# Hybrid attention and time-mix layer on one core: preparation steps joined on TensorE, attention's meta keys moved to the last key block, the next group's norm output reloaded by halves

## The chip, the core and the metric

The kernel runs on one core of a Trainium2 chip. The metric is the device time of one execution in microseconds (us). Three timed runs of the kernel before gave 2245.62, 2245.93 and 2246.27 us; the median, 2245.93 us, is the time before. PE is the TensorE engine, DVE VectorE, ACT ScalarE, POOL GpSimd, and SP the engine whose queue issues the DMAs.

## What is computed

One decoder layer over 1040 rows of width 1024: 16 meta rows are put ahead of 1024 input rows. A half-step SwiGLU FFN, a mixer, and a second half-step FFN follow each other, each behind an RMS norm. The mixer projects the normed rows once; one half of the columns feeds stick-breaking attention with 8 heads, the other an RWKV-7 time mix with 8 heads. All is fp32.

```python
h = h + 0.5 * swiglu(rms_norm(h, ffn1_norm), ...)
proj = rms_norm(h, mix_norm) @ w_in
sb_out = stick_breaking_attention(q, k, v)        # A[t,s] = sigmoid(z_ts) * prod_{s<j<t} (1 - sigmoid(z_tj))
rw_out = rwkv7_time_mix(proj[..., 3 * SB_WIDTH:]) # S = S * w + sa (kk*a) + v k ; y = S r ; per head norm, bonus, gate
h = h + concat([sb_out, rw_out]) @ w_out
h = h + 0.5 * swiglu(rms_norm(h, ffn2_norm), ...)
out = rms_norm(h, final_norm)[:, N_META:]
# in the time mix: kk = k * k_k, divided by its norm per head of 64 columns
```

## The kernel before, in words

Rows are worked on in two groups: group A holds the meta rows and the first 512 rows (528 columns, since the tensors lie transposed, depth on the partitions), group B the other 512. Every large product is made in three fp32r matmuls of high and low parts (`mm3`, L687: weights high by input high, high by low, low by high). A weight block of 512 KB is loaded into a ring of two raw buffers (`wraw`), split by ACT into its high part (`whi`) and by DVE into its low part (`wlo`), each in a ring of two. In the order of the program: FFN 1 on A, projections of A, FFN 1 on B, projections of B, output projection (`wout`, matmuls into `pwo`) of A, FFN 2 on A, output projection of B, FFN 2 on B. This is the dense work, and it keeps PE supplied.

The mixer's small work runs beside it. For each group there are four units of the time mix: two stretches of 256 or 320 rows by two pairs of heads. One unit goes through `prep` (L1373: low-rank products into `psw` and `psa`, sums of squares into `pss`, their reciprocal roots spread over the partitions by the transposes `pri`, decay factors, the products `pG`, the bonus `pb`, transposes `pT` and `pV`), `lanes` (L1568: POOL inverts 16x16 triangles into `T`; they go through memory by `Td` and `Nd` and come back by sixteen small loads into `t` and `tt`, then PE combines them: `pw`, `pp`, `pz`, `pe`), `chain` (L1657: the recurrence, 64 rows a step: `px`, `us`, `pu`, `rsv`) and `post`. Attention follows in `attn`: `attn_z` makes the weights, `attn_av` (L1897) transposes them by blocks of keys (`pat`), splits them (`ath`, `atl`) and multiplies by the values (`po`). The 16 meta keys are a block of their own, with which `attn_av` begins.

What sets the order: the whole program is written out by a planner (class `Clock`, L192). Each piece of work is a generator; where it yields, the planner may go on with another one, whichever can start earliest by the planner's own costs. So PE's order is a mix of dense work and small pieces, decided at build time; every engine then takes its instructions strictly in that order. On DVE, ACT, POOL and SP the planner picks, among pending instructions, the one that can start first, and among equals the one of higher level (`trace`, L314: URGENT, LOAD, PLAIN, LAZY; an instruction that is neither urgent nor a weight load or split has PLAIN). `prep` runs as a task of priority 6, `lanes` of 7, `chain` of 9. Where the planner sees an idle stretch on PE it can put in `warm` matmuls of the identity, which compute nothing that is kept.

`prep` and `post` share a ring of two PSUM banks (`G`, GB = 2). `need(..., bank=...)` waits for one free bank of a ring, `two(..., bank=...)` for both.

The norm output of group B is made early and parked in memory (`nbd`). When the projections of A have read a range of columns of the tiles `nh`, `nl` for the last time, `load_n1` (L2420) loads B's columns over them: two depth halves q (tiles numbered 144 and 146 for depth 0 to 511, 145 and 147 for the rest), a high and a low part each. `proj` (L1213) calls it after the last item of a range; the last three items of the projections go over the ranges (0, 256) and (256, 528) one after the other, so their weights are loaded twice.

All instructions are issued through one wrapper, so each has line L107 in the profile; they are told apart by the names of their tiles, out<-in.

Of the kernel before, what the change touches and what calls it, by code (L numbers as in the profile page):

```python
# [7 lines left out]
F32 = mybir.dt.float32  # L8
# [8 lines left out]
P = 128  # L17
# [8 lines left out]
C = 64  # L26
# [165 lines left out]
class Clock:  # L192
# [121 lines left out]
    def trace(self, eng, op, call, out, ins, k):  # L314
# [4 lines left out]
        lvl = self.LOAD if self.ahead else self.URGENT if self.urg > 0 else self.LAZY if self.urg < 0 else self.PLAIN  # L319
# [159 lines left out]
class Ker:  # L479
# [733 lines left out]
    def proj(self, items, g, before=None, after=None):  # L1213
# [7 lines left out]
        for i, (c0, c1) in enumerate(ranges):  # L1221
            if before:
                yield from before(i)
            for col0, ncol, evac in items:
                if i == 0 or len(items) > 1:
                    wh, wl = yield from load(col0, ncol)
                yield self.need(*[x[k][:, c0:c1] for k in range(KT) for x in (nh, nl)], bank=self.nextbank)
                ps = self.bank("pd")[0:ncol, :c1 - c0]
                for k in range(KT):
                    self.mm3(ps, wh[:, k, :], wl[:, k, :], nh[k][:, c0:c1], nl[k][:, c0:c1], k == 0, k == KT - 1)  # L1230
                    yield
                yield lambda: all(self.flags.get(("root", g, r)) for r in range(1 if c1 == 256 else 2))
                with self.urgent():
                    evac(ps, c0, c1)
# [116 lines left out]
    def projections(self, g, before, after):  # L1351
# [9 lines left out]
        yield from self.proj(sb[-NL:], g, None, after)  # L1361
# [11 lines left out]
    def prep(self, u, pr, out):  # L1373
# [37 lines left out]
        for e, hp in enumerate(hps):  # L1411
            nc.scalar.activation(sq[:, e, :], kS[:, e, :], AF.Square, scale=self.v("kk", hp))
        for e, hp in enumerate(hps):
            yield self.two(tw, bank=bank)
            pw, pa = G("psw")[:, :ns], G("psa")[:, :ns]
# [11 lines left out]
        blks = [(0, 0), (P, P), (ns - P, 2 * P)][:-(-ns // P)]  # L1427
        nq = 2 * len(blks)
        yield self.need(sq, bank=bank)
        ps = G("pss")  # L1430
        for e in range(2):
            for j, (t0, _) in enumerate(blks):
                k = 2 * (e * len(blks) + j)
                nc.tensor.matmul(ps[:, k:k + 2], lhsT=sq[:, e, t0:t0 + P], rhs=self.blk, start=True, stop=True)
        rt = rp.tile([P, 3, 2 * nq], F32, tag="rt", bufs=2, name="rt")
        ssv, rinv = rt[:, 0], rt[:, 1]
        V.tensor_copy(out=ssv, in_=ps[:, 0:2 * nq])
# [10 lines left out]
        for e, hp in enumerate(hps):  # L1448
            yield self.need(rw, bank=bank)
            ps = G("pri")[:, :ns]  # L1450
            for j, (t0, c0) in enumerate(blks):
                k = 2 * (e * len(blks) + j)
                rr = slice(c0 - t0, P)
                nc.tensor.transpose(out=ps[:, c0:t0 + P], in_=rw[rr, k:k + 2, :].rearrange("p a d -> p (a d)"), identity=self.ident[rr, rr])
            V.scalar_tensor_tensor(kkn[:, e, :], kS[:, e, :], self.v("kk", hp), ps, ALU.mult, ALU.mult)
# [66 lines left out]
        yield self.need(prod, bank=bank)  # L1522
        pb = G("pb")
        po = ns - 256
# [4 lines left out]
        bon = rp.tile([P, 8], F32, tag="bon", bufs=2, name="bon")  # L1529
        nc.scalar.activation(bon, pb[:, 0:8], AF.Copy)  # L1530

# [8 lines left out]

        rsv = rp.tile([P, 2, NC, 2, C], F32, tag="rsv", bufs=self.rb, name="rsv")
        vt = rp.tile([P, 4, P], F32, tag="vt", bufs=2, name="vt")
        b0 = NC - 4
        yield self.need(vS, bank=bank)
        pt = G("pV").rearrange("p (j t) -> p j t", t=P)
        for j in range(4):
            t0 = po + P * (j % 2)
            nc.tensor.transpose(out=pt[:, j, :], in_=vS[:, j // 2, t0:t0 + P], identity=self.ident)
        nc.scalar.activation(vt, pt, AF.Copy)
        for h in range(2):  # L1550
            ro = slice(64 - 64 * h, 128 - 64 * h)
            for e in range(2):
                nc.scalar.activation(rsv[ro, :, b0 + e:NC:2, h, :],
                                     pt[64 * e:64 * e + 64, :, 64 * h:64 * h + 64].rearrange("p (a b) t -> p a b t", a=2), AF.Copy)
        if b0:
            yield self.need(vS, bank=bank)
            pt = G("pV0").rearrange("p (j t) -> p j t", t=P)
            for e in range(2):
                nc.tensor.transpose(out=pt[0:64, e, :], in_=vS[:, e, 0:C], identity=self.ident)
            for h in range(2):  # L1560
                ro = slice(64 - 64 * h, 128 - 64 * h)
                nc.scalar.activation(rsv[ro, :, 0, h, :], pt[0:64, 0:2, 64 * h:64 * h + 64], AF.Copy)
# [334 lines left out]
    def attn_av(self, hp, pr, g, bufs, ops, att):  # L1897
# [10 lines left out]
        grps = [[0]] + [list(range(j, min(j + 2, nb - 1))) for j in range(1, nb - 1, 2)] + [[nb - 1]]  # L1908

        def tr(grp, h):  # L1910
            m = len(grp)
            pt = psa.tile([P, 2, 256], F32, tag="t", bufs=bufs["t"], name="pat")
            ath = ap.tile([P, 2, 256], F32R, tag="ath", bufs=bufs["at"], name="ath")
            atl = ap.tile([P, 2, 256], F32R, tag="atl", bufs=bufs["at"], name="atl")
            self.hold((ath, atl))
            ks = blocks[grp[0]][1]
            cs = slice(P, 256) if grp[0] == nb - 1 else slice(0, 256)
            for jj, j in enumerate(grp):
                s0 = blocks[j][0]
                for e in range(cs.start // P, 2):  # L1920
                    nc.tensor.transpose(out=pt[0:ks, jj, e * P:e * P + P], in_=att[e][h][:, s0:s0 + ks], identity=self.ident)
            self.split(ath[0:ks, 0:m, cs], atl[0:ks, 0:m, cs], pt[0:ks, 0:m, cs])
            return ath, atl, ks, cs

        def av(grp, hs):
            ks, cs = hs[0][2:]
            for jj, j in enumerate(grp):
                for h in range(2):
                    for x in range(2):
                        nc.tensor.matmul(po[:, h, cs], lhsT=vs[0:ks, j, h, :, :].rearrange("p a d -> p (a d)"),  # L1930
                                         rhs=hs[h][x][0:ks, jj, cs], start=(j + h + x == 0), stop=(j == nb - 1 and x == 1),
                                         skip_group_check=True)
            for x in hs:
                self.drop(x[0:2])

        def trs(grp):
# [3 lines left out]
            return grp, [tr(grp, h) for h in range(2)]  # L1940
        prev = yield from trs(grps[0])
        for grp in grps[1:] + [None]:

            yield self.need(*[x for hs in prev[1] for x in hs[0:2]])
# [170 lines left out]
    def body(self):  # L2115
# [300 lines left out]
        def dense():  # L2416
            ch = [(0, 512)]
            yield from firstA()

            def load_n1(i):  # L2420
                for q in range(2):
                    for j in range(2):
                        cs = slice(*chB[i])
                        with self.urgent():
# [116 lines left out]
```

## Time and profile before

| | |
|---|---|
| timed runs, median (lowest, highest) | 2245.93 us (2245.62, 2246.27) |
| the profiled execution's own time | 2247.88 us |
| its span, first to last instruction | 2246.0 us |
| DVE, ACT, POOL busy | 1547.6, 1096.6, 574.1 us |
| weight blocks loaded (512 KB each), five largest groups | 342 |
| mean granted PE clock | 0.997 |

A busy time is the union of an engine's instructions. Matmul ends are modelled and overlap, so the step from one matmul's start to the next tells what it costs, not its duration. In a timeline row the first number is the start, the second the time to the end of the merged instructions, and a bracket at the end gives the idle time before it with what ended it. A matmul on plain fp32 data counts as two instructions, one on fp32r data or a transpose as one.

### The profile page before, as it was taken

To read this page: it belongs to the slowest core of one execution; us is meant where nothing else is said; L and a number is where in the kernel's file an instruction comes from. 1 tells how busy PE (TensorE), PEld (TensorE's weight loads), DVE (VectorE), ACT (ScalarE), POOL (GpSimd) and SP (SyncE) were. 2 spreads that over 40 slices of the span, in tenths; PEclk is the share of its full clock that TensorE was granted. 3 is DMA by queue.
4 is the path that set the end of the run, shared out by engine and by line. 5 is a ranking of instruction groups with operands and counts; after the bars stand their busy time and mean duration, and the time that the engine had idled before them with its cause. 6 is when DMAs were issued, how large, how long until landed. Compare 5 with 4: busy or idle time off the path is not lost.

```text
span 2246.0 us, 41718 instructions
## 1 busy us (share of the span) xinstructions
PE 2218.6 (99%) x16409; PEld 1967.9 (88%) x16409; DVE 1547.6 (69%) x2633; ACT 1096.6 (49%) x2176; POOL 574.1 (26%) x722
## 2 busy tenths in 40 slices
PE   9999999999999999999999999999999999999998
PEld 8999999999878888778888988887878899899998
DVE  5887776476666655566576787556777656897774
ACT  5444444534444434655435564445656436455444
POOL 1321111013143231542012325314443101322120
PEclk9999999999999999999999999999999999999999
DMA  5543232545643232332556534334222433333332
GB/s 171 179 113 104 85 104 79 167 129 144 198 112 99 74 100 91 100 93 76 158 142 190 164 101 118 86 93 118 79 83 61 132 118 120 116 104 106 110 89 82
DMA packets 408730, 257.61 MB, mean 115 GB/s; under 512 B 45005, under 2 KB 392357, under 8 KB 408534
## 3 DMA queue, kind: packets, MB, share of 16 engines
q1 hardware_dynamic: 408534, 254.95, 39.3%
q8 instruction: 129, 2.11, 0.4%
q14 instruction: 67, 0.55, 0.1%
HBM read 220.90 MB, written 33.99 MB: 113 GB/s over the span
## 4 chain that ended last, share of the span: by engine, by line
PE 91%; DVE 3%; issue 2%; ACT 2%; DMA 1%; SPq 1%; POOL 0%; DVEq 0%; ACTq 0%; POOLq 0%
PE pd L107 33%; PE pu L107 21%; PE pg L107 21%; PE pwo L107 3%; PE px L107 3%; PE po L107 2%; PE pz L107 2%; PE pat L107 2%; DVE wlo L107 1%; SPq L107 1%; PE pG L107 1%; ACT whi L107 1%; PE psw L107 0%; PE pp L107 0%; DVE nl L107 0%
## 5 line engine op out<-in xcount | busy, mean ns | idle before, releaser
L107 ACT ACTIVATE whi<-wraw 128x1024 fp32r<-128x1024 f32 x314 | 330.7, 1053 | 324.7 <-PE pd L107 195.8
L107 DVE TENSOR_TENSOR wlo<-wraw,whi 128x1024 fp32r<-128x1024 f32 (+1 forms) x312 | 406.8, 1306 | 99.4 <-ACT whi L107 91.4
L107 PE MATMUL pd<-ah,whi 128*128 128x512 f32 (+2 forms) x944 | 323.8, 343 | 2.9 <-DVE h L107 2.0
L107 PE MATMUL pd<-ah,wlo 128*128 128x512 f32 (+2 forms) x944 | 319.3, 338 | 1.2 <-DVE wlo L107 1.2
L107 PE MATMUL pd<-al,whi 128*128 128x512 f32 (+2 forms) x944 | 317.8, 337 | 0.6 <-DVE al L107 0.3
L107 PE MATMUL pd<-nh,whi 128*128 128x256 f32 (+7 forms) x648 | 209.5, 323 | 0.0
L107 PE MATMUL pu<-nh,whi 128*128 128x512 f32 (+3 forms) x576 | 205.6, 357 | 0.0
L107 PE MATMUL pd<-nh,wlo 128*128 128x256 f32 (+7 forms) x648 | 204.3, 315 | 0.0
L107 PE MATMUL pd<-nl,whi 128*128 128x256 f32 (+7 forms) x648 | 203.4, 314 | 0.0
L107 PEld LDWEIGHTS pd<-ah,whi 128*128 128x128 f32 x944 | 177.5, 188 | 24.9 <-DVE h L107 3.4
L107 PE MATMUL pu<-nh,wlo 128*128 128x512 f32 (+3 forms) x576 | 197.9, 344 | 0.0
L107 POOL TENSOR_TENSOR qs<-wraw 128x512 f32<-128x512 f32 x64 | 106.1, 1660 | 358.1 <-DVE ql L107 133.5
L107 PE MATMUL pg<-nh,whi 128*128 128x512 f32 (+3 forms) x536 | 196.9, 367 | 0.8 <-ACT nh L107 0.6
L107 PE MATMUL pu<-nl,whi 128*128 128x512 f32 (+3 forms) x576 | 196.8, 342 | 0.0
L107 PEld LDWEIGHTS pd<-ah,wlo 128*128 128x128 f32 x944 | 177.5, 188 | 21.2 <-DVE wlo L107 2.1
L107 PEld LDWEIGHTS pd<-al,whi 128*128 128x128 f32 x944 | 177.6, 188 | 19.3 <-DVE al L107 2.0
L107 PE MATMUL pg<-nh,wlo 128*128 128x512 f32 (+3 forms) x536 | 188.7, 352 | 0.1
L107 PE MATMUL pg<-nl,whi 128*128 128x512 f32 (+3 forms) x536 | 187.6, 350 | 0.9 <-DVE nl L107 0.9
L107 DVE SCALAR_TENSOR_TENSOR h<-pd,h 128x256 f32<-128x256 f32 (+1 forms) x200 | 107.5, 541 | 76.7 <-PE pd L107 76.2
L107 POOL TENSOR_TENSOR al<-sl,ah 128x512 fp32r<-128x512 f32 (+2 forms) x45 | 73.5, 1632 | 317.7 <-ACT ah L107 314.6
L107 PEld LDWEIGHTS pd<-nh,whi 128*128 128x128 f32 (+2 forms) x648 | 120.1, 185 | 11.8 <-issue 3.1
L107 PEld LDWEIGHTS pd<-nh,wlo 128*128 128x128 f32 (+2 forms) x648 | 119.8, 185 | 8.4 <-DVE wlo L107 0.2
(395 smaller groups left out, 5633.3 us busy)
## 6 DMA issues: line engine op xcount, KB each, us to landing
wraw<-in_ffn_w_gate_dram SPq DMA_DIRECT2D x90, 512.0 KB
wraw<-in_ffn_w_up_dram SPq DMA_DIRECT2D x90, 512.0 KB
wraw<-in_ffn_w_down_dram SPq DMA_DIRECT2D x88, 512.0 KB
wraw<-in_w_in_dram SPq DMA_DIRECT2D x54, 512.0 KB
wraw<-in_w_out_dram SPq DMA_DIRECT2D x20, 512.0 KB
s<-rkvd SPq DMA_DIRECT2D x18, 256.0 KB
raw<-qkvd SPq DMA_DIRECT2D x16, 264.0 KB
raw<-qkvd SPq DMA_DIRECT2D x16, 256.0 KB
```

The source lines that it names most:

```text
L107: self._c.trace(self._n, op, lambda: f(*a, **k), out, [x for x in args if isinstance(x, bass.AP)], k)
```

## The change

Four edits:

1. Instructions of `prep` that are not urgent get the level LOAD in the place of PLAIN.
2. `prep` asks for PE three times less in a unit. The sums of squares go into the right end of the first `psa` bank, ahead of the first `psw` and `psa` products, and their tile `pss` is gone. The transposes of both halves into `pri` stand in one step that wants both banks. The bonus `pb` and the transposes `pV` of the values stand in one step that wants both banks, ahead of `pT`; the extra transposes of the very first rows, which had a bank of their own, go into the free end of `pb`.
3. `attn_av` no longer begins with the meta keys: they form the last group together with the last key block, in the other half of its tiles. The transposes of both heads of a group stand together, ahead of the splits.
4. The first depth half of B's norm output is loaded in the middle of the last projection of a range (after depth block 3 of 8), the second half after it.

```diff
-        lvl = self.LOAD if self.ahead else self.URGENT if self.urg > 0 else self.LAZY if self.urg < 0 else self.PLAIN
+        lvl = self.LOAD if self.ahead else self.URGENT if self.urg > 0 else self.LAZY if self.urg < 0 else self.LOAD if T.prio == 6 else self.PLAIN
...
     def proj(self, items, g, before=None, after=None, mid=None):
...
                     self.mm3(ps, wh[:, k, :], wl[:, k, :], nh[k][:, c0:c1], nl[k][:, c0:c1], k == 0, k == KT - 1)
+                    if mid and k == KT // 2 - 1 and (col0, ncol) == items[-1][0:2]:
+                        mid(i)
...
         for e, hp in enumerate(hps):
-            yield self.two(tw, bank=bank)
+            yield self.two(*([tw] if e else [tw, sq]), bank=bank)
+            pw, pa = G("psw")[:, :ns], G("psa")
+            pa, ps = pa[:, :ns], pa[:, 512 - 2 * nq:]
+            for j in range(0 if e else nq):
+                t0 = blks[j % len(blks)][0]
+                nc.tensor.matmul(ps[:, 2 * j:2 * j + 2], lhsT=sq[:, j // len(blks), t0:t0 + P], rhs=self.blk, start=True, stop=True)
...
+            if e == 0:
+                V.tensor_copy(out=ssv, in_=ps)
...
-        yield self.need(sq, bank=bank)
-        ps = G("pss")
...
-        for e, hp in enumerate(hps):
-            yield self.need(rw, bank=bank)
-            ps = G("pri")[:, :ns]
+        yield self.two(rw, bank=bank)
+        pri = [G("pri")[:, :ns] for e in range(2)]
+        for e, ps in enumerate(pri):
...
-        yield self.need(prod, bank=bank)
-        pb = G("pb")
+        yield self.two(prod, vS, bank=bank)
+        pb, pt = G("pb"), G("pV").rearrange("p (j t) -> p j t", t=P)
...
-        grps = [[0]] + [list(range(j, min(j + 2, nb - 1))) for j in range(1, nb - 1, 2)] + [[nb - 1]]
+        grps = [list(range(j, min(j + 2, nb - 1))) for j in range(1, nb - 1, 2)] + [[nb - 1, 0]]
+        part = lambda grp: [(0, [nb - 1], slice(P, 256)), (1, [0], slice(0, 256))] if 0 in grp else [(0, grp, slice(0, 256))]
...
+            def load_half(i, q=0):
+                for j in range(2):
+                    cs = slice(*chB[i])
+                    with self.urgent():
+                        nc.sync.dma_start(out=n[2 + j][q][:, :, cs].bitcast(F32), in_=self.nbd[j, :, 4 * q:4 * q + 4, cs])
+
             def load_n1(i):
-                for q in range(2):
-                    for j in range(2):
...
+                load_half(i, 1)
...
-            yield from self.projections(0, wait("nm0"), load_n1)
+            yield from self.projections(0, wait("nm0"), load_n1, load_half)
```

Since the planner writes the whole order anew, the edits move instructions far from their own lines. Both programs have the same number of matmuls (14767) and of the other engines' instructions. Three places follow.

DVE, the end of `prep`'s products in the very first unit (`pG` are the products, `ab`, `x` and `bg` what the mask makes of them, `qst` a projection's result). Before:

```order
L107 TENSOR_TENSOR ab<-pG,maskG 64x128
L107 TENSOR_TENSOR x_6378<-pG,maskG 64x2x64
L107 TENSOR_TENSOR wlo<-wraw,whi 128x1024
L107 TENSOR_TENSOR bg<-pG,maskG 128x2x64
L107 TENSOR_TENSOR ab<-pG,maskG 64x128
L107 TENSOR_TENSOR x_6379<-pG,maskG 64x2x64
L107 TENSOR_TENSOR qst<-pd,root 128x256
L107 TENSOR_TENSOR bg<-pG,maskG 128x2x64
```

and of the change:

```order
L107 TENSOR_TENSOR ab<-pG,maskG 64x128
L107 TENSOR_TENSOR x_6332<-pG,maskG 64x2x64
L107 TENSOR_TENSOR bg<-pG,maskG 128x2x64
L107 TENSOR_TENSOR ab<-pG,maskG 64x128
L107 TENSOR_TENSOR x_6333<-pG,maskG 64x2x64
L107 TENSOR_TENSOR qst<-pd,root 128x272
L107 TENSOR_TENSOR bg<-pG,maskG 128x2x64
L107 TENSOR_TENSOR wlo<-wraw,whi 128x1024
```

The weight split `wlo` has gone from between the masks to behind them.

PE, from the end of the projections of A to the first FFN matmul of B (`pd` is the last projection, `pg` the first gate). Before:

```order
L107 MATMUL pd<-nh_145,whi 128x272
L107 MATMUL pd<-nl_147,whi 128x272
L107 MATMUL pd<-nh_145,wlo 128x272
L107 MATMUL pu<-us,tt 128x64 x2
L107 MATMUL warm<-ident 128x128 x4
L107 MATMUL px<-rsv,bg 128x64 x4
L107 MATMUL warm<-ident 128x128
L107 MATMUL pg<-nh_144,whi 128x256
```

and of the change:

```order
L107 MATMUL pd<-nh_145,whi 128x272
L107 MATMUL pd<-nl_147,whi 128x272
L107 MATMUL pd<-nh_145,wlo 128x272
L107 MATMUL warm<-ident 128x128 x2
L107 MATMUL pu<-us,tt 128x64 x2
L107 MATMUL pg<-nh_144,whi 128x256
```

Two `warm` matmuls stand there instead of five, and a step of the recurrence has moved into the gates.

ACT and SP, inside the output projection of A, where the second unit of group B passes through `lanes`. ACT before, then of the change (`lw` is the copy of `pw` that the matmuls `pp` read):

```order
L107 ACTIVATE nh_145<-nf 128x256 x2
L107 ACTIVATE whi<-wraw 128x1024
L107 ACTIVATE nsq<-h 128x256
L107 ACTIVATE lw<-pw 128x128
L107 ACTIVATE prod<-s_14814,vec 128x256 x2
```

```order
L107 ACTIVATE nsq<-h 128x256
L107 ACTIVATE whi<-wraw 128x1024
L107 ACTIVATE lw<-pw 128x128
L107 ACTIVATE nh_145<-nf 128x256 x3
L107 ACTIVATE nsq<-h 128x256
```

SP before (the fourteen small loads `t`, `tt` that go on here, then two blocks of `w_out`), then of the change:

```order
L107 DMA wraw<-in_w_out_dram 128x8x128 x4
L107 DMA mixd_4_79<-yt 128x256
L107 DMA mixd_5_80<-yt 128x256
L107 DMA Td<-T 64x256
L107 DMA Nd<-lt 64x256
L107 DMA t_15244<-Td 16x8x16 x2
L107 DMA tt<-Nd 16x8x16 x2
```

```order
L107 DMA wraw<-in_w_out_dram 128x8x128 x6
L107 DMA Td<-T 64x256
L107 DMA Nd<-lt 64x256
L107 DMA t_15160<-Td 16x8x16 x2
L107 DMA tt<-Nd 16x8x16 x2
```

The two stores `mixd` have left the place ahead of `Td`; they now stand behind the small loads and the first of the two `w_out` blocks. On ACT nothing stands any more between that block's `whi` and `lw`, and `lt<-T`, which `Nd` waits for, stands right behind `rw`, where two other instructions were between them. On PE two blocks of `pwo`, 48 matmuls, are still to come behind `pp` in both orders; between `pw` and `pp` stood 6 `pwo`, now 24. Of `warm` matmuls both programs have 17: before, 8 at the start, 5 at the place above, 3 in this output projection and 1 behind it; in the change 8, 2, 7 and none.

More of the change, by code (lines that the diff above doesn't have):

```diff
@@ L1210, in quad, with proj @@
         return out
-    def proj(self, items, g, before=None, after=None):
+    def proj(self, items, g, before=None, after=None, mid=None):
         nh, nl = self.n[0:2]
@@ L1349, in plan, with projections @@
         yield from ffn("ffn2", wx=True, fast=True)
-    def projections(self, g, before, after):
+    def projections(self, g, before, after, mid=None):
         F = self.flags
@@ L1360, in projections @@
             yield from self.proj([it], g)
-        yield from self.proj(sb[-NL:], g, None, after)
+        yield from self.proj(sb[-NL:], g, None, after, mid)
         self.drop((self.root,))
@@ L1539, in prep @@
             nc.scalar.activation(bg[:, c0:c1, 0:4:3, :], pt[:, 0:c1 - c0], AF.Copy)
[L1541 to L1562, printed above, removed]
         pc = rp.tile([P, Q], F32, tag="pc", bufs=2, name="pc")
@@ L1906, in attn_av @@
         nb = len(blocks)
-        grps = [[0]] + [list(range(j, min(j + 2, nb - 1))) for j in range(1, nb - 1, 2)] + [[nb - 1]]
[L1910 to L1923, printed above, removed]
@@ new lines, in attn_av, with tr @@
+        part = lambda grp: [(0, [nb - 1], slice(P, 256)), (1, [0], slice(0, 256))] if 0 in grp else [(0, grp, slice(0, 256))]
+        def tr(grp):
+            pts = [psa.tile([P, 2, 256], F32, tag="t", bufs=bufs["t"], name="pat") for h in range(2)]
+            hs = [[ap.tile([P, 2, 256], F32R, tag=t, bufs=bufs["at"], name=t) for t in ("ath", "atl")] for h in range(2)]
+            for x in hs:
+                self.hold(x)
+            for j0, js, cs in part(grp):
+                for h, pt in enumerate(pts):
+                    for jj, j in enumerate(js, j0):
+                        s0, ks = blocks[j]
+                        for e in range(cs.start // P, 2):
+                            nc.tensor.transpose(out=pt[0:ks, jj, e * P:e * P + P], in_=att[e][h][:, s0:s0 + ks], identity=self.ident)
+            for h, pt in enumerate(pts):
+                for j0, js, cs in part(grp):
+                    x = slice(0, blocks[js[0]][1]), slice(j0, j0 + len(js)), cs
+                    self.split(hs[h][0][x], hs[h][1][x], pt[x])
+            return hs
@@ new lines, in av @@
+        def av(grp, hs):
+            for j0, js, cs in part(grp):
+                for jj, j in enumerate(js, j0):
+                    ks = blocks[j][1]
+                    for h in range(2):
+                        for x in range(2):
+                            nc.tensor.matmul(po[:, h, cs], lhsT=vs[0:ks, j, h, :, :].rearrange("p a d -> p (a d)"),
+                                             rhs=hs[h][x][0:ks, jj, cs], start=(j == 1 and h + x == 0), stop=(j == 0 and x == 1),
+                                             skip_group_check=True)
@@ L1933, in av @@
             for x in hs:
[L1934 removed]
+                self.drop(x)
         def trs(grp):
```

49 lines of the change are left out of this document (25 added, 24 removed).

## The prediction

> **What bounds the kernel now.** The first view is the page's table of engines:
>
> ```profile
> PE 2218.6 (99%) x16409; PEld 1967.9 (88%) x16409; DVE 1547.6 (69%) x2633; ACT 1096.6 (49%) x2176; POOL 574.1 (26%) x722
> ```
>
> PE is busy for 2218.6 of 2246.0 us. So no change of order can win more than 27 us, unless it makes PE's own steps shorter or its clock higher. The change removes no matmul. What can move is PE's waits, the price of its switches between kinds of matmuls, and the clock. The list of waits on PE, longest first, tells where the idle time sits:
>
> ```profile
> PE pp L107 <- issue: 2.7, 1, 2.7
> PE pg L107 <- DMA g1r<-in_ffn_norm_dram: 2.4, 1, 2.4
> ```
>
> All rows of that list sum to 18.7 us in 31 waits (total, times, longest). Beside the one at the program's start only `pp` waits longer than 1 us at a time. I looked at that one in the timeline, then at the place where `pb` waits, then at the start of B's FFN, where `warm` matmuls hide idle time from that list.
>
> **The long wait, in the output projection of A.** PE and ACT around it:
>
> ```profile
> 1301.61 0.38 PE L107 MATMUL warm<-ident 128*128 128x128 f32 x2
> 1304.64 0.65 PE L107 MATMUL pp<-tt,lw 32*16 32x16 f32 x62 [2.66 <-issue]
> 1303.02 1.06 ACT L107 ACTIVATE whi<-wraw 128x1024 fp32r<-128x1024 f32 x1 [0.60 <-DMA wraw<-in_w_out_dram]
> 1304.29 0.26 ACT L107 ACTIVATE lw<-pw 128x128 f32<-128x128 f32 x1
> ```
>
> "Issue" is not the cause. `pp` reads `lw`, and `lw` stands on ACT behind a weight copy `whi`, which waited for its block to land, at about 1302.95. Why was the block late? SP's rows say it:
>
> ```profile
> 1283.88 0.98 SPq L107 DMA_DIRECT2D mixd<-yt  x2
> 1284.90 0.51 SPq L107 DMA_DIRECT2D Td<-T  x1
> 1288.31 0.47 SPq L107 DMA_DIRECT2D Nd<-lt  x1
> 1288.88 1.01 SPq L107 DMA_DIRECT2D t<-Td  x2
> 1296.77 1.68 SPq L107 DMA_DIRECT2D tt<-Nd  x1
> 1298.56 1.02 SPq L107 DMA_DIRECT2D wraw<-in_w_out_dram  x2
> ```
>
> Sixteen small loads take SP from 1288.88 to 1298.45, 9.6 us, and the block is issued behind them. After the wait the clock falls. Here is the granted clock in the stretch behind it, then two neighbouring steps at that clock and two at the full one:
>
> ```profile
> 1305.30:1312.00 6.70, 6.70 (x61) 6.54 (x54) 4.42 (x7) 2.58 (x8) 4.96 (x5) 0.50 0.55 159
> 1309.20 0.41 PE L107 MATMUL pwo<-nh,wlo 128*128 128x256 f32 x1
> 1309.41 0.41 PE L107 MATMUL pwo<-nh,whi 128*128 128x256 f32 x1
> 1301.25 0.28 PE L107 MATMUL pwo<-nh,whi 128*128 128x256 f32 x1
> 1301.37 0.28 PE L107 MATMUL pwo<-nl,whi 128*128 128x256 f32 x1
> ```
>
> The step is 0.21 us at clock 0.50 and 0.12 at full clock, so 6.7 us hold what 3.8 would: 2.9 lost, beside 2.66 of waiting. The place costs 5.6 us.
>
> What the change does there: `Td` no longer stands behind the two stores, and `Nd` waits for a copy `lt` that the new order puts right behind `rw`:
>
> ```profile
> 1285.76 0.63 ACT L107 ACTIVATE rw<-rt 128x512 f32<-128x512 f32 x1 [0.92 <-DVE rt L107]
> 1287.65 0.63 ACT L107 ACTIVATE lt<-T 64x256 f32<-64x256 f32 x1
> 1279.96 0.21 POOL L107 TENSOR_TENSOR T<-T,ltmp 64x15 f32<-64x15 f32 x1
> ```
>
> `rw` ends at 1286.39 and `T` is done at 1280.17, so `lt` can run at 1286.4 in place of 1287.65: `Nd`, the sixteen loads and the block come 1.25 us earlier, and the block lands at 1301.7. Then `whi` takes 1.06 and `lw`, now directly behind it, 0.26 us: `pp` starts at about 1303.2. PE reaches `pp` at 1302.0 as before. The wait is 1.2 us in place of 2.66: **1.4 us saved**. Does the clock still fall? The trace has one wait of 0.98 us (`pb`, below) with no fall behind it and one of 2.66 with a fall; 1.2 is near the first, so I take **2.9 us saved** as well, and keep 0 as the other end.
>
> The Trainium skill, "TensorE: Matmul & The Clock Gate", section "What's actually happening", has the clock halved after an idle window of about 3.4 us, on a window that runs freely. This trace differs: 2.66 us were enough. By the page's figure the new wait of 1.2 us would keep the clock too, and the sum stays; by its free window the fall could come in some executions and not in others, and then the three runs before, which lie within 0.65 us, would differ by some 3.
>
> Against this the new order puts seven `warm` matmuls into that stage in place of three. Four of them are the `warm` row of the next block with x8; they run from 574.23 to 575.34, 0.28 us each. Where they stand PE is idle beside them too: there five of them and 0.70 us of waiting fill 2.0 us, 0.4 each. So four more cost 1.1 to 1.6 us, I take **1.6**, and the one that stood behind this stage and is gone gives **0.3** back. Sum of the place: -1.4 - 2.9 + 1.6 - 0.3 = **-3.0 us**, with ends at +1.3 (nothing saved, the `warm` paid) and -5.9 (wait and clock gone, only the 0.3 beside it).
>
> **From the projections to B's FFN.**
>
> ```profile
> 573.73 0.66 PE L107 MATMUL pu<-us,tt 128*128 128x64 f32 x4
> 574.23 1.11 PE L107 MATMUL warm<-ident 128*128 128x128 f32 x8
> 576.03 1.10 PE L107 MATMUL px<-rsv,bg 128*128 128x64 f32 x8 [0.70 <-DVE rsv L107]
> 576.98 0.44 PE L107 MATMUL warm<-ident 128*128 128x128 f32 x2
> 577.17 0.36 PE L107 MATMUL pg<-nh,whi 128*128 128x256 f32 x1
> 560.00:565.00 5.00, 5.00 (x42) 4.95 (x42) 4.74 (x10) 3.55 (x9) 0.00 (x0) 1.00 1.07 335
> 565.00:570.00 5.00, 5.00 (x43) 4.84 (x42) 3.32 (x9) 1.71 (x6) 0.00 (x0) 1.00 1.12 339
> ```
>
> From 574.23 to 577.17 PE does one useful thing, the 0.95 us of `px`; 2.0 us are lost. The stretches ahead (last numbers: share of the DMA engines, GB/s) show why: the DMA engines are full, with the reloads of `nh`, `nl` and the weights in one queue. The first gate's weights come last. In the change the first reloads start twelve matmuls earlier (12 x 0.125 = 1.5 us), two `warm` stand there, 0.6 us, and `px` has moved into the gates. I take 2.0 - 0.6 = **1.4 us saved**, between 0 and 2.0. The reload itself was not late: its first range was issued at 558 to 561 us. What it is moved past is one block of `w_in`, now behind two reloads of 512 KB, 3.1 us at 335 GB/s. Its cover:
>
> ```profile
> 562.76 1.06 ACT L107 ACTIVATE whi<-wraw 128x1024 fp32r<-128x1024 f32 x1 [0.18 <-PE pd L107]
> ```
>
> This is the last projection's weights, split at 562.76; that projection is the last 24 steps of 0.125 us ahead of 573.73, so it began near 570.7, some 8 us later, or a little before, for the recurrence's pieces between them. The split waited for PE to leave its buffer, not for the landing. 3.1 us fit. Cost 0.
>
> **The first `pb`.**
>
> ```profile
> 508.87 2.35 POOL L107 TENSOR_TENSOR bk<-bk,pe 128x1280 f32<-128x1280 f32 x1 [23.18 <-PE pG L107]
> 509.42 2.88 DVE L107 TENSOR_TENSOR wlo<-wraw,whi 128x1024 fp32r<-128x1024 f32 x1
> 512.77 1.02 PE L107 MATMUL pb<-blk,prod 128*128 128x2 f32 x8 [0.98 <-DVE bg L107]
> 513.52 0.27 DVE L107 TENSOR_TENSOR bg<-pG,maskG 128x128 f32<-128x128 f32 x1
> ```
>
> `pb` waits for a bank that the masks on DVE must leave, and the masks stood behind a weight split that took 2.88 us beside POOL's `bk`. The joined step wants **both** banks, an added wait: in the old order it would have had to wait for the last `bg`, to 513.79, 1.0 us longer, with all projections queued behind it on PE. In the new order the six masks and one `qst` come first, some 6 x 0.29 + 0.41 = 2.2 us from the 508.8 of the first, 511.0, and `pb` is due at 511.8 (512.77 less its wait). **1.0 us saved**, at worst 1.0 lost. In the seven other units `pb` waits for nothing worth a row in the list, and at least as much stands between `pG` and it in the new order as in the old.
>
> **Switches on PE.** Counted in the two orders, runs of plain fp32 or transposes between fp32r matmuls fall from 348 to 322, 12 of the 26 fewer being plain fp32. Changes of the array's row or column size stay, 346 and 347. What a run costs:
>
> ```profile
> 1270.84 0.95 PE L107 MATMUL pss<-blk,sq 128*128 128x2 f32 x8
> 1271.65 0.36 PE L107 MATMUL pwo<-nh,whi 128*128 128x256 f32 x1
> 1271.85 0.28 PE L107 MATMUL pwo<-nl,whi 128*128 128x256 f32 x1
> 921.00 0.60 PE L107 MATMUL pat<-ident,sg 128*16 128x128 f32 x4
> 921.36 0.48 PE L107 MATMUL pg<-nh,whi 128*128 128x512 f32 x1
> 921.67 0.40 PE L107 MATMUL pg<-nl,whi 128*128 128x512 f32 x1
> 936.12 1.04 PE L107 MATMUL pat<-ident,sg 128*128 128x128 f32 x8
> ```
>
> The first matmul behind `pss` takes 0.20 us to the next in place of 0.12: 0.08 a run, less the shorter end of the run itself. I take 0.06 x 12 = **0.7 us saved**. For attention the four meta transposes alone take 0.36 us and 0.08 behind them, 0.44; inside the longer row four take half of 0.96, 0.48. So the sixteen merges of edit 3 give **0**, though they look like the largest edit. Ends: 26 x 0.08 = 2.1 us gained; or, as the 16-row `po` behind 128-row `po` is in no row and a change of size costs some 0.1, 1.6 lost.
>
> **The level of `prep`** costs nothing directly: DVE, ACT and POOL have 31, 51 and 74% of the span free. What it pushes back is `lanes` on POOL, whose `T` was done at 1280.17 and stored only at 1284.90: 4.7 us of cover.
>
> **The sum.** -3.0 - 1.4 - 1.0 - 0.7 = -6.1. I looked up the waits that the change reaches; of those it makes I see none, though the order is redrawn from 450 us on. The 28 smaller waits hold 14 us, 0.5 each; I add two, 1.1. That makes -5.0. The profiled execution took 2247.88 us, 1.88 around its span, and stands 1.95 above the median; the places are the same, so I take the sum from the median: 2245.93 - 5.0 = **2240.9 us**, 0.22% less. A measurement can tell about 0.2% from no change, 4.5 us, so the forecast lies at that edge.
>
> **Rivals.**
> - *The long wait stays.* The block is still behind sixteen loads, and `lw` is tied to it more tightly. If it lands as late as before, wait and half clock stay, four `warm` are paid: -6.1 + 4.3 + 1.1 = -0.7, **2245.2**. For it: nothing shortens the 9.6 us of SP. Against: `Nd` is freed earlier.
> - *More goes than I count.* The long wait vanishes whole (-1.2) and every saved run pays (-1.4), with no new waits added: -6.1 - 2.6 = -8.7, **2237.2**.
> - *Slower: a joined step stops PE.* A step that wants both banks waits for all masks on DVE; if a weight split as slow as the 2.88 us above falls ahead of the last one, PE waits. It decides where the wait reaches the 2.66 us behind which the clock fell: 2.66 + 2.9 = 5.6 us. With the long wait still there: -0.7 + 5.6 = +4.9, **2250.8**. For it: one unit's `pb` did wait behind such a split. Against: 15 matmuls or more lie between `pG` and `pb` in all eight.
> - *The transfer was hidden anyway.* B's reload was early; if the weights don't come earlier either, the 1.4 us stay: 2242.3. This lies in the forecast's own range, 2238 to 2243.5.
>
> **Chances.** Forecast 0.50 (0.37 of it under 2241.4, the edge), the long wait stays 0.30, more goes 0.10, slower 0.10. Faster by over 0.2%: 0.37 + 0.10 = 0.47; within: 0.13 + 0.30 = 0.43; slower: 0.10. The range reaches from below the second rival's 2237.2 (the 0.6 of `warm` at B's FFN and 1.1 of the others gone too) to beyond the first one's 2245.2 (its switches at the dear end, 1.6 + 0.7): 2235.5 to 2247.5. It leaves out the slower case and the far ends, under 2 in 10.
>
> **What would show it.** In the list of waits, `pp` under 1.5 us or gone and no stretch at clock 0.50 in the output projection (right), or `lw` again behind a late `whi` (wrong). `pb` near 512 us without a bracket. From the last `pd` of A's projections to the first `pg` of B 1.1 us, `pu` included. Transposes `pat` of 128 columns at 0.11 to 0.12 us each. A second stretch at clock 0.50, or a new wait over 2 us, would make the forecast wrong upwards.

## The result, and the profile after

The changed kernel took 2257.2 us, median of 5 runs (2255.8 to 2258.4); the kernel before, run beside it, 2246.3 (2245.6 to 2248.7). The ratio is 1.0042 (95% interval 1.0031 to 1.0054): slower by about 0.4%, where 0.2% faster was forecast. The profiled execution took 2255.8 us with a span of 2253.8, against 2246.0.

First the page's table of engines and three rows of the list of PE's waits (total, times, longest) of the changed kernel:

```profile
PE 2218.9 (98%) x16409; PEld 1972.8 (88%) x16409; DVE 1553.0 (69%) x2633; ACT 1095.4 (49%) x2176; POOL 572.5 (25%) x722
PE px L107 <- DVE rsv L107: 4.3, 9, 2.5
PE pwo L107 <- DVE wlo L107: 3.4, 3, 2.4
PE pp L107 <- issue: 0.6, 1, 0.6
```

PE's busy time has not moved (2218.6 before), so the 7.8 us of span are waits. All rows of the list sum to 26.5 us in 45 waits; before it was 18.7 in 31. `pp` has fallen from 2.7 to 0.6, the way that was forecast, and two waits about as long as the old one stand in its place: `pwo` for `wlo`, and `px` for `rsv`. Not all of the 7.8 us belong to the change: 1.1 are waits of `pxn` and `px` near 22 and 24 us, where both orders are still the same. They come and go between executions; `norm_held` below has 1.75 us there, `both_mended` none.

Busy time hides one more loss, the clock. The two stretches at half clock of the changed kernel, from the view of windows (after the length, each engine's busy time and instructions; at the end the granted clock, DMA share, GB/s):

```profile
1307.30:1314.00 6.70, 4.35 (x21) 4.27 (x21) 5.79 (x6) 1.88 (x5) 4.55 (x4) 0.50 0.36 104
1327.80:1337.90 10.10, 7.51 (x34) 7.33 (x35) 7.33 (x18) 6.00 (x17) 1.80 (x3) 0.50 0.19 54
```

Up to half of the 4.35 + 7.51 us that PE is busy there is lost, 5.9 us; before, one stretch with 6.70 busy lost up to 3.35. So 7.8 us more waiting and some 2.6 more at half clock, 10.4 together, make a span 7.8 longer: the other 2.6 us were won, by shorter steps on PE.

**Where `pwo` waits.** PE, ACT, SP and DVE in the output projection, to be held against the rows of the forecast:

```profile
1304.24 0.65 PE L107 MATMUL pp<-tt,lw 32*16 32x16 f32 x62 [0.64 <-issue]
1309.73 0.58 PE L107 MATMUL pwo<-nh,wlo 128*128 128x256 f32 x1 [2.35 <-DVE wlo L107]
1287.44 0.63 ACT L107 ACTIVATE rw<-rt 128x512 f32<-128x512 f32 x1 [0.72 <-DVE rt L107]
1302.92 1.06 ACT L107 ACTIVATE whi<-wraw 128x1024 fp32r<-128x1024 f32 x1 [0.25 <-DMA wraw<-in_w_out_dram]
1303.89 0.26 ACT L107 ACTIVATE lw<-pw 128x128 f32<-128x128 f32 x1
1288.64 0.47 SPq L107 DMA_DIRECT2D Nd<-lt  x1
1298.59 0.39 SPq L107 DMA_DIRECT2D wraw<-in_w_out_dram  x1
1305.46 0.47 DVE L107 SCALAR_TENSOR_TENSOR nf<-h,vec,ny 128x256 f32<-128x256 f32 x1
1307.39 4.49 DVE L107 TENSOR_TENSOR wlo<-wraw,whi 128x1024 fp32r<-128x1024 f32 x2
1307.15 1.44 POOL L107 TENSOR_TENSOR a<-a,kkn 128x512 f32<-128x512 f32 x1
1308.55 2.25 POOL L107 TENSOR_TENSOR prod<-prod,kp 128x512 f32<-128x512 f32 x1
```

The block of `w_out` is issued at 1298.59, where it was 1298.56 before: nothing came earlier. `Nd` does follow `rw` more closely, but `rw` itself runs 1.68 us later than before. `pp` waits less because PE arrives later, 1303.6 for 1302.0: 24 `pwo` stand between `pw` and `pp` in this order, where 6 stood before. Then `whi` is done at 1303.98, and its partner `wlo` starts at 1307.39: DVE's order has `nf`, `nl` and `h` ahead of it. Beside POOL's `a` and `prod` two `wlo` take 4.49 us (at 1283.82, with POOL idle, one takes 1.22). The late start and the slow split are the 2.35 us of `pwo`.

**Where `px` waits.** PE behind the last gate matmul of the first half:

```profile
1324.04 1.00 PE L107 MATMUL px<-rsv,bg 128*128 128x64 f32 x8
1324.88 0.66 PE L107 MATMUL nyp<-ident,fst 128*128 128x128 f32 x4
1325.72 0.43 PE L107 MATMUL px<-rsv,x 128*128 128x64 f32 x2 [0.18 <-DVE rsv L107]
1326.36 0.88 PE L107 MATMUL px<-rsv,x 128*128 128x64 f32 x6 [0.20 <-DVE rsv L107]
1327.92 1.12 PE L107 MATMUL pu<-us,tt 128*128 128x64 f32 x4 [0.68 <-ACT us L107]
1331.50 1.97 PE L107 MATMUL px<-rsv,bg 128*128 128x64 f32 x8 [2.47 <-DVE rsv L107]
1333.23 0.56 PE L107 MATMUL pu<-nh,whi 128*128 128x256 f32 x1
```

and the same place before:

```profile
1321.05 1.00 PE L107 MATMUL px<-rsv,bg 128*128 128x64 f32 x8
1322.30 0.28 PE L107 MATMUL pu<-nh,whi 128*128 128x256 f32 x1
1323.36 1.00 PE L107 MATMUL px<-rsv,x 128*128 128x64 f32 x8
1324.40 0.71 PE L107 MATMUL nyp<-ident,fst 128*128 128x128 f32 x4
```

Before, the up matmuls `pu<-nh` begin behind the gate and fill PE between the recurrence's steps. In the change `nyp`, the norm of the second half, comes ahead of them. It takes the PSUM bank that `pu` would have had, and the norm's `nf` takes the buffer (tag `sl`, a ring of two) that the gate's result `sl` needs. So, by this reading of the order, `pu` cannot start, and `px`, `px`, `pu`, `px` stand side by side: each waits for copies of the one before on ACT and DVE, where the norm's `nf` and `nh` are ahead. For the longest of these waits, on DVE:

```profile
1328.30 1.59 DVE L107 SCALAR_TENSOR_TENSOR nf<-h,vec,ny 128x256 f32<-128x256 f32 x4
1331.16 0.28 DVE L107 COPY rsv<-pu 64x128 f32<-64x128 f32 x1
```

The four brackets make 3.5 us, and the clock is at 0.50 from 1327.7 on.

### The profile page after: what moved, and what is told of

Its sections match the earlier page's. It is cut to its first block, busy times and chain, and to the rows that moved or that the text cites. A ratio compares the mean times of both kernels' runs of the same rounds, so it can differ in the third digit from the quotient of the medians.

```text
span 2253.8 us, 41762 instructions
## 1 busy us (share of the span) xinstructions
PE 2218.9 (98%) x16409; PEld 1972.8 (88%) x16409; DVE 1553.0 (69%) x2633; ACT 1095.4 (49%) x2176; POOL 572.5 (25%) x722
## 4 chain that ended last, share of the span: by engine, by line
PE 89%; DVE 4%; ACT 3%; DMA 2%; issue 1%; POOL 0%; SPq 0%; DVEq 0%; ACTq 0%; POOLq 0%
PE pd L107 32%; PE pu L107 21%; PE pg L107 20%; PE pwo L107 3%; PE px L107 3%; PE po L107 2%; PE pz L107 2%; PE pat L107 2%; ACT whi L107 1%; DVE wlo L107 1%; PE pG L107 1%; DMA wraw<-in_w_in_dram 1%; DMA wraw<-in_ffn_w_gate_dram 0%; PE psw L107 0%; ACT nh L107 0%
```

## The experiments

**First: which edit brings this in?** Each was undone alone. `no_level` undoes

```diff
-        lvl = ... else self.LAZY if self.urg < 0 else self.LOAD if T.prio == 6 else self.PLAIN
+        lvl = ... else self.LAZY if self.urg < 0 else self.PLAIN
```

> The change without the level of the preparation (the joins, attention and halves stay). Theory: the loss sits in A's output projection and the start of its FFN, where the new order puts two dependent steps of the recurrence (px, pu, px) side by side on PE with no gate matmul between them; here the order has gates between them, so no stretch at clock 0.50 behind 1325 us. But without the level the preparation of B's later units is late, and in this order PE runs out of FFN blocks ahead of the second output projection (near 1860 to 1920 us): waits of 5 us or more there, 2255 to 2270 us in all. Rival (the level is what costs): both half-clock stretches go and the time is 2246 or less.

`no_joins` gives `pss`, both `pri`, `pb`, `pV` and `pV0` their own steps again, as

```diff
-        yield self.two(prod, vS, bank=bank)
-        pb, pt = G("pb"), G("pV").rearrange("p (j t) -> p j t", t=P)
+        yield self.need(prod, bank=bank)
+        pb = G("pb")
```

> The change without the joined steps (level, attention, halves stay). Theory: with the joins undone the order keeps gate matmuls between the recurrence's steps; the second stretch at clock 0.50 (10.2 us) goes, the first in the output projection may stay: 2243 to 2249 us. Rival (the level moves the order and the joins are innocent): the px wait of 2.5 us and its half clock stay, 2254 to 2259.

`no_attention` puts the meta keys first again, `no_halves` reloads the norm output whole behind the last projection:

```diff
-        grps = [list(range(j, min(j + 2, nb - 1))) for j in range(1, nb - 1, 2)] + [[nb - 1, 0]]
+        grps = [[0]] + [list(range(j, min(j + 2, nb - 1))) for j in range(1, nb - 1, 2)] + [[nb - 1]]
```

```diff
-            yield from self.projections(0, wait("nm0"), load_n1, load_half)
+            yield from self.projections(0, wait("nm0"), load_n1)
```

> The change without attention's meta keys at the end. Theory: the place with px, pu, px side by side is in this order as well, so a px wait of 2 to 3 us behind 1325 us and a stretch at clock 0.50 behind it: 2252 to 2259 us. Rival (attention's new order costs, or shifts the place): 2245 to 2249.

> The change without the reload by halves. Theory: the same px wait of 2 to 3 us with clock 0.50 behind it, 2252 to 2259 us. Rival (the halves shift B's start and all that follows): no such wait, 2245 to 2249.

| run | us, median | ratio to before (95% interval) |
|---|---|---|
| no_level | 2267.0 | 1.0089 (1.0068 to 1.0110) |
| no_joins | 2247.2 | 1.0003 (0.9993 to 1.0012) |
| no_attention | 2258.3 | 1.0050 (1.0034 to 1.0066) |
| no_halves | 2259.6 | 1.0056 (1.0035 to 1.0078) |

The long `px` wait for `rsv` on DVE is there without attention and without the halves, and goes without the joins or without the level. The list of PE's waits, a row of `no_attention`, then one of `no_joins`, then two of `no_level`:

```profile
PE px L107 <- DVE rsv L107: 4.7, 9, 2.9
```

```profile
PE px L107 <- DVE rsv L107: 1.0, 4, 0.4
```

```profile
PE pwo L107 <- DVE wlo L107: 9.6, 7, 5.1
PE px L107 <- DVE rsv L107: 2.1, 7, 0.6
```

So in the changed kernel this wait comes with joins and level together. The joins without the level are worse still: `pwo` waits up to 5.1 us at a time, at 1886 us. The four times came as the theory said (`no_halves` 0.6 us beyond its range), from two runs each for `no_level` and `no_halves` and three for `no_attention`; against its theory `no_level` has a stretch at clock 0.50 behind 1325 us, at 1407, after `pu` has waited 1.6 us for `us`. That `no_joins` is level with before, and not faster, is taken up below.

**Second: are those two places the loss?** `split_first` keeps the changed kernel's order but for one instruction. When the planner gives out a certain `nl`, the late `wlo` is given out first:

```diff
+        for d in self.pend["v"] if o.seq == 12720 else ():
+            if d.seq == 12711:
+                d.call()
+                d.call = lambda: None
         o.call()
```

> The changed kernel in its own order but for one instruction: on DVE the late wlo of the output projection (the one pwo waits 2.35 us for) stands ahead of three nl/nf of the norm and not behind them. Theory A (the wait makes the clock fall): wait and half-clock stretch of 6.8 us both go, 2.35 + 2.2 us for the 4.5 us of work at half clock: 2252 to 2254. Theory B (the clock is set on a grid of 3.4 us by the work of the piece before, and had fallen 0.1 us before that wait began): the stretch stays in the profile and only 1 to 1.5 us are won, 2255 to 2257. The px wait behind 1325 us stays in both.

`norm_held` lets the second norm go on to `nyp` only when `pu` has its bank:

```diff
             ps = bank(name)[:, :c1 - c0]
+            if name == "pu" and nm == "ffn2":
+                self.flags["up0"] = True
...
         yield from self.room(self.fp, *rings)
+        if hold:
+            yield hold
         yield self.need(st[:, 1], bank=next or self.nextbank)
```

> The changed kernel with one wait added in program order: the norm of the second half of A's FFN (nyp and its nf) is held until the up matmuls pu of the first half have taken their bank. Theory (nyp took the bank and nf the buffer that the gate's sl and pu needed, so px, pu, px stood side by side on PE): gates and ups stand between the recurrence's steps again, no px wait over 1 us behind 1325 us, no stretch at clock 0.50 there; 2.5 + 0.7 us of waits and some 3.9 of half clock go: 2249 to 2252. Rival (the recurrence's chain is late itself, whatever stands between): the wait moves to another place of this stage, 2255 to 2259.

`both_mended` has both edits.

> Both edits in one kernel: the split first and the norm held. Theory: both added waits and the second half clock go, 2244 to 2249, by theory A for the clock 2244 to 2246 and by B 2247 to 2249. It is the test of whether these two places are all that the forecast missed: with its other steps right, 2241 to 2246. Rival (other places lose as well): over 2250.

| run | us, median | ratio to before (95% interval) |
|---|---|---|
| split_first | 2254.5 | 1.0027 (1.0018 to 1.0036) |
| norm_held | 2251.0 | 1.0012 (1.0003 to 1.0020) |
| both_mended | 2249.6 | 1.0005 (0.9996 to 1.0014) |

The kernel before, beside these runs, took 2248.3 us, 2 more than beside the change, so the ratios are what to compare. `split_first` came between its two theories, `norm_held` as its theory had it. `both_mended` is 0.6 us above its range, and well above the 2241 to 2246 by which these two places would be all that the forecast missed. By ratios `split_first` gives back 0.0015, 3.4 us; `norm_held` 0.0030, 6.7 us; both 0.0037, 8.3 of the 9.4 us that 1.0042 stands for. By the intervals each of these is good to some 3 us: the gain of `norm_held` and of both is clear, that of `split_first` lies at the edge. PE in `norm_held`, at the place where `px`, `px`, `pu`, `px` stood side by side (the first rows of runs of 9 to 12 gate and up matmuls among them):

```profile
1324.91 1.00 PE L107 MATMUL px<-rsv,bg 128*128 128x64 f32 x8
1325.72 0.37 PE L107 MATMUL pu<-nh,whi 128*128 128x256 f32 x1
1327.22 1.13 PE L107 MATMUL px<-rsv,x 128*128 128x64 f32 x8
1328.19 0.66 PE L107 MATMUL nyp<-ident,fst 128*128 128x128 f32 x4
1330.10 0.66 PE L107 MATMUL pu<-us,tt 128*128 128x64 f32 x4 [0.15 <-DVE us L107]
```

Of 3.5 us of waits 0.15 are left, with no stretch at clock 0.50 there. So `nyp` and its `nf` ahead of `pu` were the cause; whether the bank or the buffer, the edit doesn't tell, since it frees both. And 6.7 us is a net figure: the planner draws the order anew from 1325 us on, and part of the waiting comes back later, as the rival had it. At 1347.6 `pu` waits 1.64 us for `us`, and the clock falls behind it for 3.41 us; at 1471.3 `pp` waits 2.31. `both_mended` has the same two waits:

```profile
1342.95 0.66 PE L107 MATMUL pu<-us,tt 128*128 128x64 f32 x4 [1.63 <-ACT us L107]
1465.02 0.48 PE L107 MATMUL pp<-lw,tt 32*32 32x16 f32 x18 [2.25 <-issue]
```

Between 1340 and 1500 us its waits sum to 4.8 us, with 3.41 us at clock 0.50; before, to 1.5, with none; in the change to 3.8, with none.

`split_first` also tells how the clock falls. Its first stretch:

```profile
1306.30:1309.60 3.30, 2.95 (x14) 2.95 (x15) 2.05 (x3) 3.16 (x8) 2.81 (x3) 0.50 0.54 153
```

The `wlo` wait of 2.35 us is gone, and the clock still falls, at 1306.24; but for 3.41 us and not for 6.83. So the fall was there ahead of that wait, as theory B had it. Whether the wait then kept the clock down for a second piece is not shown: before, the clock stayed down for 6.83 us with PE busy all through, and in `only_halves` (below) for 3.41 at the same place. The 3.4 us won lie at A's lower end, and the interval reaches B's 1 to 1.5 too.

**Third: the price of the old place, and what is still missing.** `before_block_first` takes the kernel before and issues the late `w_out` block ahead of the last three small loads (the same four lines as above, on SP's list); `all_mended` does so in `both_mended`.

> The kernel before, in its own order but for one DMA: the late w_out block of the output projection is issued on SP ahead of the last three of the sixteen small t and tt loads, 1.8 us earlier. It measures by itself the place that the forecast priced at 5.6 us (2.66 of wait, 2.9 of half clock). By that price: the pp wait shrinks from 2.66 to some 0.7 us and the clock falls less often there, 2 to 4.5 us less, ratio 0.998 to 0.999. Rival (the wait only moves on to pwo, whose wlo is late on DVE behind the norm, as in the changed kernel): ratio 0.9995 to 1.0005 with a wait of pwo for wlo in the list.

> The changed kernel with the split first, the norm held and, in place of a late w_out block behind sixteen small loads, the block ahead of the last three of them, 1.4 us earlier. If the three places are what keeps the change from paying: 1 to 2 us below both_mended, ratio to before 0.999 to 1.000. If not, as both_mended, 1.0005, and what is missing to the forecast sits elsewhere.

`before_block_first` came to 0.9997 (0.9989 to 1.0006), `all_mended` to 1.0011 (1.0000 to 1.0021): neither won anything. The first has the time of its rival, but not its way: `pwo` waits for `wlo` no more than before, 1.4 us. ACT in `before_block_first`:

```profile
1302.60 0.81 ACT L107 ACTIVATE nh<-nf 128x256 fp32r<-128x256 f32 x2 [0.49 <-DVE nf L107]
1303.32 1.04 ACT L107 ACTIVATE whi<-wraw 128x1024 fp32r<-128x1024 f32 x1
1304.57 0.26 ACT L107 ACTIVATE lw<-pw 128x128 f32<-128x128 f32 x1
```

`whi` no longer waits for the block, and starts no earlier: it stands behind two `nh`, which wait for `nf` on DVE. The wait of `pp` went from 2.66 to 1.94 us. So the late block carried 0.6 to 0.7 us of that wait (the 0.60 in `whi`'s bracket before said so), and ACT's own queue the rest. The lateness itself was a chance of that one profile: in `only_attention`, `only_halves` and `attention_halves`, where the block still stands behind the sixteen loads, `whi` doesn't wait for it either, and `pp` waits 1.94 us in each.

**Fourth: each part by itself**, on the kernel before.

> The kernel before with attention's meta keys at the end alone. Forecast's term: 0, between 2.1 less and 1.6 more. Since the order up to B's start is as before but for attention's own steps, and px, pu stay apart behind 1325 us: ratio 0.999 to 1.001. Rival (a redrawn order costs, whatever redraws it): 1.002 or more.

> The kernel before with the reload by halves alone. Forecast's term: the start of B's FFN 1.4 us earlier (0 to 2.0), ratio 0.9990 to 1.0000, with five warm matmuls at that place down to two or none. Rival (the reload was not what the start waited for, the last projections' weights or the recurrence's rsv are): the waits there move to pu and px, ratio 1.0000 to 1.0010.

> The kernel before with the preparation at the loads' level alone. Forecast's term: 0, free engines hide it. By the other runs' sum it costs: no_joins holds level, attention and halves and stands at 1.0003, where the last two alone would give 0.997: ratio 1.002 to 1.004, with new waits of PE for DVE or ACT. If it costs nothing, 0.999 to 1.001, and the gains do not add up.

> The kernel before with the first join alone (sums of squares ahead of the sigmoids). If a join costs by itself: 1.001 to 1.004, with px or pu waiting over 1 us behind 1325 us. If the joins cost only together with the level: 0.999 to 1.001.

> The kernel before with the last join alone (pb, pV and pV0 in one step). Forecast's term: the pb wait near 512 us gone, 1.0 us less, and a third of the 0.7 us of switches: 0.9990 to 1.0000. If the order that it redraws costs: 1.001 to 1.004.

`attention_halves` leaves level and joins out; `no_join_a` is the change with the join of `pss` alone undone.

> The kernel before with attention's meta keys at the end and the reload by halves; no level, no joins. If the gains add up: 0.9979 and 0.9991 give 0.9970, near 2241 us. Rival (the gains were luck of a redrawn order and not of the steps themselves): 0.999 to 1.001.

> The change with the first of the three joins undone (pss is its own step again; pri, pb with pV, level, attention and halves stay). Theory: this join, which puts the sums of squares ahead of the sigmoids, moves the preparation enough to swap nyp and pu; without it nyp comes behind pu again in this order, so no px wait over 1 us behind 1325: 2246 to 2252. Rival (the later joins do it): the px wait stays, 2254 to 2259.

The edits are those of the change's diff, in these selections. The last two columns are the mean granted clock over all runs of the row, and of the kernel before beside them:

| run | us, median | ratio to before (95% interval) | clock | clock of before |
|---|---|---|---|---|
| only_attention | 2243.6 | 0.9979 (0.9970 to 0.9988) | 0.9971 | 0.9969 |
| only_halves | 2246.7 | 0.9991 (0.9982 to 1.0000) | 0.9956 | 0.9969 |
| attention_halves | 2243.5 | 0.9987 (0.9978 to 0.9996) | 0.9949 | 0.9975 |
| only_level | 2252.3 | 1.0022 (1.0013 to 1.0032) | 0.9942 | 0.9975 |
| only_join_a | 2251.7 | 1.0016 (1.0007 to 1.0026) | 0.9947 | 0.9975 |
| only_join_c | 2256.6 | 1.0042 (1.0027 to 1.0058) | 0.9953 | 0.9975 |
| no_join_a | 2250.9 | 1.0014 (1.0004 to 1.0024) | 0.9956 | 0.9966 |

Three expectations were missed. `only_attention` gains 4.7 us where none was expected, `attention_halves` less than the two together, and `only_join_c`, from four runs, costs where its term was a gain. Attention alone is a version to keep: 0.2% faster than before and 0.6% than the change; with the halves beside it the interval is nearly the same, so these runs don't tell the two apart. The level and each of the two joins tried cost 0.2 to 0.4% by themselves; the level's 0.0022 takes back the 0.0013 of `attention_halves`, which is why `no_joins`, with all three, stands level with before. `only_join_a` has a `px` wait of 1.8 us at 1330.8 too, without the level, and `no_join_a` none over 0.4, so the first join has the larger part in that place; but `no_join_a` has `pu` waiting 1.5 us for `tt` at 1322.4. `only_join_c` shows the trade best. Of it, `pb` and the list of waits:

```profile
513.68 1.02 PE L107 MATMUL pb<-blk,prod 128*128 128x2 f32 x8
PE pwo L107 <- DVE wlo L107: 2.6, 2, 2.1
PE pu L107 <- ACT us L107: 2.4, 6, 0.7
PE pd L107 <- DVE wlo L107: 2.2, 4, 0.8
```

`pb` waits for nothing, as the forecast had it, and `pwo`, `pu` and `pd` wait 1.2, 1.1 and 1.0 us more than before (1.4, 1.3, 1.2 there). All its waits together are 5.5 us longer.

For the halves the clock seems to take back what the waits gave. Before, PE had five `warm` matmuls at the start of B's FFN and no fall in the profile. `attention_halves` has none there, and its clock is at 0.50 from 574.8 to 578.2:

```profile
570.35 1.10 PE L107 MATMUL px<-rsv,bg 128*128 128x64 f32 x8 [0.74 <-DVE rsv L107]
571.83 1.21 PE L107 MATMUL px<-rsv,x 128*128 128x64 f32 x8 [0.38 <-DVE rsv L107]
575.78 1.81 PE L107 MATMUL px<-rsv,bg 128*128 128x64 f32 x8
```

That can be why the two gains did not add up to the 0.9970 expected. For it speaks a count over all the profiles. Six of these kernels have no `warm` matmul between 560 and 590 us (`only_halves`, `attention_halves`, `only_level`, `only_join_c`, `no_joins`, `no_join_a`), and in all six the clock falls there, for 3.4 to 17.1 us; the twelve others have two or five, and it falls in one of them, `all_mended`. It is not shown: the orders differ in more than that, and a version with the halves and with `warm` matmuls kept at that place was not tried.

## Why the prediction was wrong

- **The new waits, sized at 1.1 us: the step that failed.** The forecast "looked up the waits that the change reaches; of those it makes I see none", and put 1.1 us for a redrawn order. Mending two places alone gives back 8.3 us, so these waits and the half clock behind them were the term that was missing. The rival on the other side had the mechanism's kind right, a new wait that brings the clock down, and its place wrong: not a joined step that waits for both its banks, but work of the norm and of FFN that the joins and the level moved past each other, 800 us later.
- **The output projection, -3.0.** The wait of `pp` fell by 2.0 us, not 1.4, and for another reason: the step "the sixteen loads and the block come 1.25 us earlier" did not happen, since `rw`, `Nd` and PE all came late together; nor does "PE reaches `pp` at 1302.0 as before" hold, with 18 `pwo` more in between. And the block was only in part the releaser: in the order of before it held 0.6 of the 2.66 us, and ACT's two `nh` the rest. The half clock stayed. Sum of the place: 2.0 saved, 2.35 of a new wait.
- **The start of B's FFN, -1.4, and `pb`, -1.0.** `pb` waits no more, as forecast. Behind the last projection PE now has

```profile
579.31 0.61 PE L107 MATMUL warm<-ident 128*128 128x128 f32 x4
580.49 0.66 PE L107 MATMUL pu<-us,tt 128*128 128x64 f32 x4 [0.57 <-DVE us L107]
581.99 1.10 PE L107 MATMUL px<-rsv,bg 128*128 128x64 f32 x8 [0.44 <-DVE rsv L107]
```

  the reload is no longer what is late; the recurrence's copies are. And ahead of it, at 479 and 486 us, `pd` waits anew for `st` on DVE, 1.7 us in the list (2 times, 1.1 at most). Of the 2.4 us forecast for this part of the program, and a share of the switches' 0.7, 0.8 came: from 440 to 1055 us the same `pd` matmuls stand 0.81 us closer together.
- **Attention, 0.** It was worth 0.2%, 4.7 us by its ratio (2.7 to 6.7 by the interval): the forecast's own end of 2.1 gained was too near. It counted the transposes `pat` and left out `po`. Before, a meta group's `po` most often ends a run, with dense work behind it:

```profile
925.20 0.27 PE L107 MATMUL po<-atl,vs 16*128 16x256 f32 x1
925.40 0.50 PE L107 MATMUL pu<-nh,whi 128*128 128x512 f32 x1
925.73 0.40 PE L107 MATMUL pu<-nl,whi 128*128 128x512 f32 x1
925.96 0.40 PE L107 MATMUL pu<-nh,wlo 128*128 128x512 f32 x1
```

  the matmul behind it takes 0.33 us to the next in place of 0.23. Before, a dense matmul of 512 columns stands behind 14 of the 16 such groups, in `only_attention` behind 5: some 0.9 us. The runs of `pat` and `po` themselves fall from 88 to 72 and take 0.5 us less in sum, 88.1 for 88.6. Another 1.2 is a wait of `pd` for `wlo` near 1750 us (2 times, 0.8 at most), which is in the list of before and not in that of `only_attention`. In the two stretches in which attention runs, 906 to 1044 and 1560 to 1772 us, the same dense matmuls stand 1.2 and, with that wait, 2.5 us closer together; for the rest of the 4.7 the traces show no cause.
- **The level, nothing.** That DVE, ACT and POOL are idle a quarter to three quarters of the span says nothing of who comes first in them at one moment. It costs 0.2%, and its clock is the lowest in the table, 0.9942.

What stays open: `both_mended` stands 0.27%, 6 us, above the forecast, and holds 4.7 us of attention that the forecast had not, so some 11 us went elsewhere. By themselves the level (0.22%, 4.9 us), the first join (3.6) and the last (9.4) show that they lose as much. The waits of `both_mended` between 1340 and 1500 us, 3.4 us more than before and a stretch at half clock, are one place of it; in the changed kernel `pyT` waits 1.69 us for `y` there, at 1461.5. The others were not taken apart, and the join of `pri` was not run alone.

## What to carry to other kernels

Where one planner draws the whole order, an edit's price is not the sum of its own instructions: read the new order itself for places where dependent steps stand side by side on the engine that bounds the kernel, with no independent work between them. Such a place shows before any run, and here mending one gave back more than all the edits were meant to win. Try each edit alone: of the four, attention paid, the halves paid 0.1% at the edge of the noise, and the level and the joins hid it. When a bracket names the last of several releasers, look at what else is queued ahead of the instruction, before a gain is counted for that one.

## What the hardware showed

The clock falls on a grid. Over the traces the stretches at 0.50 inside the program last 3.41, 6.83, 10.24 and 17.07 us, one, two, three and five times 3.41. A wait need not fill such a piece: in the change one stretch follows a piece with waits of 0.64 and 0.48 us, short `pp` and `warm`; the next follows a piece with some 0.8 us of waits between `px`, `nyp` and `pu`. And which places fall differs between runs of one kernel: the wait of 0.98 us at `pb` had no fall behind it in the profile of before, but 3.41 us of it in those of `before_block_first` and `only_halves`, whose order is the same up to there. The forecast's argument "0.98 without a fall" rested on one execution's chance.

The Trainium skill, "TensorE: Matmul & The Clock Gate", section "What's actually happening", gives a window of 3413 ns that runs freely and explains by it why the point at which the clock changes varies; the lengths here agree. It has the clock fall after a whole idle window; here a partly busy one was enough.

The clock also goes with most of the scatter between runs. The 33 runs of the kernel before beside `split_first`, by their granted clock:

| granted clock | runs | mean us |
|---|---|---|
| 0.999 | 2 | 2245.3 |
| 0.998 | 4 | 2246.4 |
| 0.997 | 8 | 2247.3 |
| 0.996 | 16 | 2249.1 |
| 0.995 | 3 | 2252.3 |

The means at the ends of this table lie 0.3% apart, so a change of 0.2% in this kernel can't be read from two single runs, and a single profile shows one case of the clock.
